# A two-layer encoder on one core: the casts, sums and embedding weights around the down projection, and when the first transposes follow

## The chip, the cores and the metric

The kernel runs on one core of a Trainium2 chip. Its time is device microseconds of one execution of the whole program; a version's time is the median of several runs. The engines are TensorE (PE in the profile, its weight loads PEld), VectorE (DVE), ScalarE (ACT), GpSimd (POOL) and SyncE (SP), which issues the transfers. Each engine takes its own instructions in the order of the program and waits on semaphores for what other engines make.

## What is computed

Two layers of an encoder on 1024 tokens of width 1024 in float32. The first layer's mixer is a pair of attentions, the second's a differential attention. The parts that the change touches come behind the mixer:

```python
def conv_ffn(x, w_gate, w_up, conv_w, conv_b, w_down):
    a = x @ w_gate
    u = x @ w_up
    ...
    return (jax.nn.gelu(c) * u) @ w_down      # c: a convolved over 3 tokens

x = layer_norm(ALPHA * x + mixer(x))
x = layer_norm(ALPHA * x + conv_ffn(x))
x = x + sigmoid(x @ W_g) * (p[i] @ W_p)       # the embedding step
```

The inner width of the feed-forward part is 2816, so w_down is 2816x1024: 22 blocks of 128 rows.

## The kernel before

Float32 products are made of rounded halves. A value is split into a hi part, which is a cast to a shorter format, and a lo part, the value less its hi part; `mm3` (lines 159 to 161) issues three matmuls, hi by hi, hi by lo and lo by hi. So each operand needs one cast (on ACT or POOL) and one subtraction (line 142, DVE, `lo_part`; line 149 in `split`).

**The down projection** (class `Down`) uses seven half-sized products instead of eight: `DOWN` lists them, a00, s4, a01, s2, s3, s1, a11. The left operand gr (combined gated activations, prepared before and kept in DRAM) and the right one wd (a block of w_down or a sum of two) are multiplied over nh = 11 blocks for each of the seven, so 77 products n per layer. A product is four blocks t of 128 tokens by 512 columns, three matmuls 128x512 each, so 12 matmuls. `run` goes through n in order; at n it issues the product's matmuls, then sums of weights for n + 5 (`draw`), then at most two steps that read a finished group's banks into xn (`read`, lines 1180 to 1201), then the operands of n + 3 (`prep`, AHEAD = 3): the cast of gr to gd (line 1149, ACT), the cast of wd (line 1150, through `pool_copy` at line 139, POOL), and two lo parts (line 142, DVE). `add` (line 319, DVE) makes the sums of weights in place, for s4 and a01 inside `prep`, for s2 and s3 in `draw`. gr comes by DMA on SP, two products in one transfer, into two buffers (`load_g`, line 1126). The operands gd and wd live in buffers for three products.

The last three products (74 to 76) are issued together for each token block: at n = 74 the loop goes over t, and for each t over the three products, so that the banks of a token block are done early.

**The embedding step** (class `Embedding`) is prepared beside the last group of products: `beside(f)` is called at the end of step f of group 6. It fetches the eight blocks of its weights (wgr), splits them into wgh and wgl (line 146 cast on ACT, line 149 lo part on DVE for even blocks and on POOL for odd ones), takes the statistics and the norm of the first token blocks (lines 892 to 897 statistics, 902 to 904 the norm's three steps), and at f = 7 puts the first transposes (`turn(0)`: eight matmuls by the identity at line 164, a cast at line 289 on ACT and lo parts on DVE). The products with W_g (pg) come behind the projection.

The order on each engine is set when the program is built: a scheduler takes the work that is ready by its costs and priorities, and an instruction named in `keep_in_program_order` stays where the program text has it. Step 74's loop is written before its `beside`, and f = 7 belongs to step 73, so the transposes stand ahead of product 74.

Of the kernel before, what the change touches and what calls it, by code (L numbers as in the profile page):

```python
# [12 lines left out]
ALU = mybir.AluOpType  # L13
# [4 lines left out]
NK = 8  # L18
NF = 22
# [13 lines left out]
def tile_hybrid_encoder(  # L33
# [32 lines left out]
    nc = tc.nc  # L66
# [61 lines left out]
    def f32(ap):  # L128
        return ap.bitcast(F32)
# [8 lines left out]
    def pool_copy(o, i):  # L138
        nc.gpsimd.tensor_scalar(o, i, 1.0, 1.0, op0=ALU.mult, op1=ALU.mult)  # L139
# [176 lines left out]
            return self.h[t][:, k, :], self.l[t][:, k, :]  # L316

    def add(o, a, b, op=ALU.add, eng=None):
        (eng or nc.vector).tensor_tensor(f32(o), f32(a), f32(b), op=op)

    def split_value(v, h, l, hi=None):
        if hi is nc.gpsimd:
# [776 lines left out]
    class Down:  # L1099
# [29 lines left out]
        def draw(self, n):  # L1129

            if n >= self.n:
                return
            q, f = DOWN[n // self.nh], n % self.nh
            b00, b01, b10, b11 = (self.b(f, kc) if f + self.nh * kc[0] in self.w else None
                                  for kc in ((0, 0), (0, 1), (1, 0), (1, 1)))
            if q == "s2":
                add(b00, b11, b00)
            if q == "s3":
                add(b10, b10, b00, ALU.subtract)

        def prep(self, n):

            if n >= self.n:
                return
            q, f = DOWN[n // self.nh], n % self.nh
            make = runit if q == "a11" else rtile
            g, w = make("gd", [P, 2, 512]), make("wd", [P, 2, 512])
            rg, rw = self.raw[n // 2][:, n % 2, :], self.b(f, self.B[q])
            nc.scalar.copy(g[:, 0], rg)  # L1149
            pool_copy(w[:, 0], rw)  # L1150
            lo_part(g[:, 1], rg, g[:, 0])
            lo_part(w[:, 1], rw, w[:, 0])
            if q == "s4":
                add(rw, rw, self.b(f, (0, 1)), ALU.subtract)
            if q == "a01":
                add(self.b(f, (0, 1)), self.b(f, (0, 1)), self.b(f, (0, 0)), ALU.subtract)
            self.op[n] = g, w
            if n % 2 == 1:
                self.load_g((n + 3) // 2)
# [60 lines left out]
        def run(self, beside):  # L1220
            nh, n_all = self.nh, self.n
            end = n_all - AHEAD
            for n in range(n_all):
                q, f = n // nh, n % nh
                if f == 0:
                    self.banks(q)
                if n < nh:
                    self.load_w(nh + n)
                if nh < n <= nh + 4:
                    residual(self.i, self.xns, n - nh - 1)  # L1230
                if 3 * nh < n <= 3 * nh + 4:
                    residual(self.i, self.xns, n - 3 * nh + 3)
                if n < end:
                    for t in range(4):
                        self.product(n, t)
                elif n == end:
                    for t in range(4):
                        for m in range(end, n_all):
                            self.product(m, t)
                        if t == 1:  # L1240
                            for step in self.read(q)[0:2]:
                                step()
                if n < end:
                    self.op.pop(n)
                self.draw(n + AHEAD + 2)
                for _ in range(2):
                    if self.todo:
                        self.todo.pop(0)()
                self.prep(n + AHEAD)
                if f == nh - 1 and q < 6:  # L1250
                    self.todo += self.read(q)
                if q == 6 and n < end:
                    beside(f)
            for step in self.read(6)[2:]:
                step()

# [262 lines left out]
    class Embedding:  # L1519
        def __init__(self, i, xns, sink):  # L1520
            self.i, self.xns, self.sink = i, xns, sink
            self.w, self.st, self.rows = [], {}, {}

        def load(self):

# [4 lines left out]
                    raw[k] = unit("wgr", [P, 1024])  # L1530
                    nc.sync.dma_start(out=raw[k], in_=w_ple[self.i, k])

            def weight(k):
                make = rtile if k < 3 else runit
                h, l = make("wgh", [P, 1024]), make("wgl", [P, 1024])
                split(raw.pop(k), h, l, nc.scalar, nc.gpsimd if k % 2 else nc.vector)
                self.w.append((h, l))

            def beside(n):
                if n == 0:  # L1540
                    self.ln = LN(ln_fg[self.i], ln_fb[self.i])
                    fetch(0)
                    fetch(1)
                if n > 0:
                    for k in ((0,), (1,), (2,), (3, 4), (5,), (6,), (7,))[n - 1] if n <= 7 else ():
                        fetch(k + 2)
                        weight(k)
                if n == 3:
                    self.stats(0, False)
                if n == 5:  # L1550
                    self.apply(0)
                if n == 6:
                    self.stats(1, False)
                if n == 7:
                    self.turn(0)
            return beside

# [162 lines left out]
```

## Time and profile before

| | |
|---|---|
| median of 3 runs | 3075.62 us (3073.82 to 3077.36) |
| the profiled execution | 3070.2 us, its span 3068.4 us |
| PE busy | 2956.1 us, 96% |
| DVE, ACT, POOL busy | 2339.5, 1239.0, 1110.6 us |
| one projection in the profile | about 1250 to 1472 us in layer 0, the like in layer 1 |

The profile is of one execution. Busy time counts instructions of an engine; where one waits, the timeline shows the idle before it in brackets with the instruction that released it. Matmuls overlap: in a full stream one starts each 0.227 us, though its row is 0.39 us long, so what a wait costs is read from start to start.

### The profile page before, as it was taken

To read this page: it belongs to the slowest core of one execution; us is meant where nothing else is said; L and a number is where in the kernel's file an instruction comes from. 1 tells how busy PE (TensorE), PEld (TensorE's weight loads), DVE (VectorE), ACT (ScalarE), POOL (GpSimd) and SP (SyncE) were. 2 spreads that over 40 slices of the span, in tenths; PEclk is the share of its full clock that TensorE was granted. 3 is DMA by queue.
4 is the path that set the end of the run, shared out by engine and by line. 5 is a ranking of instruction groups with operands and counts; after the bars stand their busy time and mean duration, and the time that the engine had idled before them with its cause. 6 is when DMAs were issued, how large, how long until landed. Compare 5 with 4: busy or idle time off the path is not lost.

```text
span 3068.4 us, 43192 instructions
## 1 busy us (share of the span) xinstructions
PE 2956.1 (96%) x15456; PEld 2535.4 (83%) x15456; DVE 2339.5 (76%) x4014; ACT 1239.0 (40%) x2652; POOL 1110.6 (36%) x1646
## 2 busy tenths in 40 slices
PE   8999999999889999999999999999998999999989
PEld 8888989887778888877788999998776888887877
DVE  6676477876898888788638777777779988879674
ACT  5555477761232222223226555555413322222221
POOL 4444544333232222234225555554333222213232
PEclk9999999999999999999999999999998999999999
DMA  3000100033223232734111100001532232255331
GB/s 122 29 28 19 38 29 8 22 118 130 96 103 103 99 106 106 283 112 168 56 59 36 35 28 29 28 18 62 174 108 86 103 103 103 103 201 198 97 137 65
DMA packets 119718, 272.14 MB, mean 89 GB/s; under 512 B 11344, under 2 KB 35024, under 8 KB 119504
## 3 DMA queue, kind: packets, MB, share of 16 engines
q1 hardware_dynamic: 119504, 269.37, 25.6%
q8 instruction: 123, 2.02, 0.3%
q14 instruction: 91, 0.75, 0.1%
HBM read 196.46 MB, written 72.88 MB: 88 GB/s over the span
## 4 chain that ended last, share of the span: by engine, by line
PE 70%; DVE 16%; issue 6%; POOL 3%; ACT 3%; DMA 2%; SPq 0%; POOLq 0%; DVEq 0%; ACTq 0%
PE xt L164 5%; PE pb L159 5%; PE pb L160 5%; PE pb L161 5%; PE pp L159 4%; PE s L588 4%; PE pp L161 4%; PE pp L160 4%; PE pd L160 2%; PE pd L161 2%; PE pd L159 2%; PE pa L159 2%; PE pg L159 2%; PE pa L161 2%; PE pa L160 2%
## 5 line engine op out<-in xcount | busy, mean ns | idle before, releaser
L142 DVE TENSOR_TENSOR ptl<-xt,pth 128x512 fp32r<-128x512 f32 (+2 forms) x384 | 239.7, 652 | 59.2 <-ACT pth L399 42.6
L159 PE MATMUL pp<-wh,xth 128*128 128x384 f32 x768 | 266.3, 347 | 7.9 <-ACT wh L146 7.4
L160 PE MATMUL pp<-wl,xth 128*128 128x384 f32 x768 | 258.8, 337 | 1.9 <-DVE wl L149 1.9
L161 PE MATMUL pp<-wh,xtl 128*128 128x384 f32 x768 | 257.9, 336 | 0.0
L440 ACT ACTIVATE e<-s,nmx 128x1024 f32<-128x1024 f32 x192 | 214.7, 1120 | 81.4 <-DVE nmx L838 58.7
L160 PE MATMUL pd<-wd,gd 128*128 128x512 f32 x616 | 242.4, 393 | 4.2 <-DVE wd L142 4.2
L159 PE MATMUL pd<-wd,gd 128*128 128x512 f32 x616 | 241.0, 391 | 0.0
L161 PE MATMUL pd<-wd,gd 128*128 128x512 f32 x616 | 240.5, 390 | 0.0
L139 POOL TENSOR_SCALAR wd<-wd 128x512 fp32r<-128x512 f32 x154 | 129.9, 848 | 290.8 <-PE pd L161 215.6
L1149 ACT CAST gd<-gr 128x512 fp32r<-128x512 f32 x154 | 94.8, 622 | 312.2 <-PE pd L161 222.0
L325 ACT CAST w<-ws 128x512 fp32r<-128x512 f32 x132 | 81.2, 621 | 336.8 <-PE pb L161 281.2
L164 PE MATMUL xt<-ident,e 128*128 128x128 f32 x1440 | 198.0, 274 | 10.0 <-POOL e L740 3.0
L159 PE MATMUL pb<-xt,w 128*128 128x512 f32 x528 | 207.0, 392 | 0.0
L160 PE MATMUL pb<-xt,w 128*128 128x512 f32 x528 | 206.5, 391 | 0.0
L161 PE MATMUL pb<-xt,w 128*128 128x512 f32 x528 | 206.3, 391 | 0.0
L139 POOL TENSOR_SCALAR w<-ws 128x512 fp32r<-128x512 f32 x44 | 33.4, 761 | 467.1 <-PE pa L161 416.9
L164 PEld LDWEIGHTS xt<-ident,e 128*128 128x128 f32 x1440 | 163.4, 141 | 30.7 <-ACT sq L870 5.9
L142 DVE TENSOR_TENSOR wd<-wd,wd 128x512 fp32r<-128x512 f32 x154 | 112.3, 731 | 68.8 <-POOL wd L139 68.8
L142 DVE TENSOR_TENSOR w<-ws,w 128x512 fp32r<-128x512 f32 x176 | 152.4, 869 | 5.2 <-ACT w L325 3.2
L159 PEld LDWEIGHTS pp<-wh,xth 128*128 128x128 f32 x768 | 144.6, 188 | 13.4 <-ACT wh L146 8.0
L838 DVE TENSOR_REDUCE nmx<-s 128x1 f32<-128x1024 f32 x128 | 150.4, 1213 | 1.7 <-PE s L588 1.6
L159 PE MATMUL pb<-xb,w 128*128 128x512 f32 x352 | 140.2, 398 | 9.8 <-DVE u L1330 5.7
(293 smaller groups left out, 8864.5 us busy)
## 6 DMA issues: line engine op xcount, KB each, us to landing
gr<-gated SPq DMA_DIRECT2D x76, 512.0 KB, 3.7
gated<-c SPq DMA_DIRECT2D x90, 256.0 KB, 3.7
wf<-in_w_gate_dram SPq DMA_DIRECT2D x44, 512.0 KB, 4.0
wf<-in_w_up_dram SPq DMA_DIRECT2D x44, 512.0 KB, 4.1
wd<-in_w_down_dram SPq DMA_DIRECT2D x44, 512.0 KB, 6.0
wr<-in_w_c_dram SPq DMA_DIRECT2D x32, 384.0 KB, 3.2
gated<-u SPq DMA_DIRECT2D x44, 256.0 KB, 2.2
pes<-peo SPq DMA_DIRECT2D x64, 128.0 KB, 1.9
```

The lines of the kernel that those rows point to most:

```text
L139: nc.gpsimd.tensor_scalar(o, i, 1.0, 1.0, op0=ALU.mult, op1=ALU.mult)
L142: nc.vector.tensor_tensor(lo, src, f32(hi), op=ALU.subtract)
L159: nc.tensor.matmul(o, lhsT=lh, rhs=rh, start=start, stop=False)
L160: nc.tensor.matmul(o, lhsT=lh, rhs=rl, start=False, stop=False)
L161: nc.tensor.matmul(o, lhsT=ll, rhs=rh, start=False, stop=stop)
L164: nc.tensor.transpose(o, in_=i, identity=ident)
L325: nc.scalar.copy(h, v)
L440: nc.scalar.activation(dst, s, AF.Exp, bias=negmax, scale=1.0, accum_out=l)
L588: nc.tensor.matmul(s[:, kh * 512:kh * 512 + 512], lhsT=qt[:, hl, i, :], rhs=self.ks[kh][:, j, :], start=hl == 0, stop=hl == 1)
L838: nc.vector.tensor_reduce(out=nmx, in_=s, axis=AX.X, op=ALU.max, negate=True)
L1149: nc.scalar.copy(g[:, 0], rg)
```

## The change

Five edits, in both layers alike. The cast of wd goes from POOL to ACT. The sums of weights are pinned to their place in the program. Weights 3 to 7 of the embedding are fetched beside group 5, and 3 to 6 split there, the rest beside group 6 at f = 0 and 2 to 4; every lo part of them is on DVE. The weights are held in a dict by their number. The transposes of the first token block are put in the last step's loop, ahead of its fourth token block.

```diff
--- before.py
+++ after.py
@@ -316,7 +316,7 @@
             return self.h[t][:, k, :], self.l[t][:, k, :]
 
     def add(o, a, b, op=ALU.add, eng=None):
-        (eng or nc.vector).tensor_tensor(f32(o), f32(a), f32(b), op=op)
+        return (eng or nc.vector).tensor_tensor(f32(o), f32(a), f32(b), op=op)
 
     def split_value(v, h, l, hi=None):
         if hi is nc.gpsimd:
@@ -1134,9 +1134,9 @@
             b00, b01, b10, b11 = (self.b(f, kc) if f + self.nh * kc[0] in self.w else None
                                   for kc in ((0, 0), (0, 1), (1, 0), (1, 1)))
             if q == "s2":
-                add(b00, b11, b00)
+                tc.keep_in_program_order(add(b00, b11, b00))
             if q == "s3":
-                add(b10, b10, b00, ALU.subtract)
+                tc.keep_in_program_order(add(b10, b10, b00, ALU.subtract))
 
         def prep(self, n):
 
@@ -1147,13 +1147,13 @@
             g, w = make("gd", [P, 2, 512]), make("wd", [P, 2, 512])
             rg, rw = self.raw[n // 2][:, n % 2, :], self.b(f, self.B[q])
             nc.scalar.copy(g[:, 0], rg)
-            pool_copy(w[:, 0], rw)
+            nc.scalar.copy(w[:, 0], rw)
             lo_part(g[:, 1], rg, g[:, 0])
             lo_part(w[:, 1], rw, w[:, 0])
             if q == "s4":
-                add(rw, rw, self.b(f, (0, 1)), ALU.subtract)
+                tc.keep_in_program_order(add(rw, rw, self.b(f, (0, 1)), ALU.subtract))
             if q == "a01":
-                add(self.b(f, (0, 1)), self.b(f, (0, 1)), self.b(f, (0, 0)), ALU.subtract)
+                tc.keep_in_program_order(add(self.b(f, (0, 1)), self.b(f, (0, 1)), self.b(f, (0, 0)), ALU.subtract))
             self.op[n] = g, w
             if n % 2 == 1:
                 self.load_g((n + 3) // 2)
@@ -1235,6 +1235,8 @@
                         self.product(n, t)
                 elif n == end:
                     for t in range(4):
+                        if t == 3:
+                            beside(nh)
                         for m in range(end, n_all):
                             self.product(m, t)
                         if t == 1:
@@ -1249,8 +1251,8 @@
                 self.prep(n + AHEAD)
                 if f == nh - 1 and q < 6:
                     self.todo += self.read(q)
-                if q == 6 and n < end:
-                    beside(f)
+                if q >= 5 and n < end:
+                    beside(f if q == 6 else f - nh)
             for step in self.read(6)[2:]:
                 step()
 
@@ -1519,7 +1521,7 @@
     class Embedding:
         def __init__(self, i, xns, sink):
             self.i, self.xns, self.sink = i, xns, sink
-            self.w, self.st, self.rows = [], {}, {}
+            self.w, self.st, self.rows = {}, {}, {}
 
         def load(self):
 
@@ -1530,28 +1532,32 @@
                     raw[k] = unit("wgr", [P, 1024])
                     nc.sync.dma_start(out=raw[k], in_=w_ple[self.i, k])
 
-            def weight(k):
-                make = rtile if k < 3 else runit
+            def weight(k, make=runit):
                 h, l = make("wgh", [P, 1024]), make("wgl", [P, 1024])
-                split(raw.pop(k), h, l, nc.scalar, nc.gpsimd if k % 2 else nc.vector)
-                self.w.append((h, l))
+                split(raw.pop(k), h, l, nc.scalar)
+                self.w[k] = h, l
 
             def beside(n):
+
+                if -11 < n < 0 and n % 2 == 0:
+                    fetch(NK + n // 2)
+                if -10 < n < -2 and n % 2 == 1:
+                    weight(NK + (n - 1) // 2)
                 if n == 0:
+                    weight(7)
                     self.ln = LN(ln_fg[self.i], ln_fb[self.i])
                     fetch(0)
-                    fetch(1)
-                if n > 0:
-                    for k in ((0,), (1,), (2,), (3, 4), (5,), (6,), (7,))[n - 1] if n <= 7 else ():
-                        fetch(k + 2)
-                        weight(k)
+                if n in (1, 2):
+                    fetch(n)
+                if n in (2, 3, 4):
+                    weight(n - 2, rtile)
                 if n == 3:
                     self.stats(0, False)
                 if n == 5:
                     self.apply(0)
                 if n == 6:
                     self.stats(1, False)
-                if n == 7:
+                if n == NF // 2:
                     self.turn(0)
             return beside
 
```

What this does to the order of each engine's instructions is seen at three places of layer 0. The first is PE at the last products: pd are the banks of token blocks, wd and gd the operands, xt the transposes' banks. Before:

```order
L159 MATMUL pd_15070<-wd_15203,gd_15202 128x512
L160 MATMUL pd_15070<-wd_15203,gd_15202 128x512
L161 MATMUL pd_15070<-wd_15203,gd_15202 128x512
L164 MATMUL xt_15305<-ident,xn_13945 128x128 x4
L164 MATMUL xt_15312<-ident,xn_13945 128x128 x4
L159 MATMUL pd_15069<-wd_15235,gd_15234 128x512
L160 MATMUL pd_15069<-wd_15235,gd_15234 128x512
```

After:

```order
L159 MATMUL pd_15096<-wd_15298,gd_15297 128x512
L160 MATMUL pd_15096<-wd_15298,gd_15297 128x512
L161 MATMUL pd_15096<-wd_15298,gd_15297 128x512
L164 MATMUL xt_15334<-ident,xn_13945 128x128 x4
L164 MATMUL xt_15341<-ident,xn_13945 128x128 x4
L159 MATMUL pd_15096<-wd_15249,gd_15248 128x512
L160 MATMUL pd_15096<-wd_15249,gd_15248 128x512
```

The eight transposes (two rows of four) stood ahead of product 74's first matmul and stand now behind three of its four token blocks, 27 matmuls later.

The second is DVE while the first sums of weights are made: line 142 are the lo parts, line 319 the sums. Before:

```order
L319 TENSOR_TENSOR wd_13683<-wd_13683,wd_13536 128x512
L319 TENSOR_TENSOR wd_13536<-wd_13536 128x512
L319 TENSOR_TENSOR wd_13536<-wd_13683,wd_13536 128x512
L142 TENSOR_TENSOR gd_13888<-gr_13829,gd_13888 128x512
L142 TENSOR_TENSOR wd_13889<-wd_13705,wd_13889 128x512
L319 TENSOR_TENSOR wd_13705<-wd_13705,wd_13538 128x512
L319 TENSOR_TENSOR wd_13538<-wd_13538 128x512
L142 TENSOR_TENSOR gd_13909<-gr_13829,gd_13909 128x512
L142 TENSOR_TENSOR wd_13910<-wd_13725,wd_13910 128x512
L319 TENSOR_TENSOR wd_13538<-wd_13705,wd_13538 128x512
L319 TENSOR_TENSOR wd_13725<-wd_13725,wd_13554 128x512
L319 TENSOR_TENSOR wd_13554<-wd_13554 128x512
```

After, once each sum is pinned:

```order
L142 TENSOR_TENSOR gd_14003<-gr_13916,gd_14003 128x512
L142 TENSOR_TENSOR wd_14004<-wd_13809,wd_14004 128x512
L319 TENSOR_TENSOR wd_13809<-wd_13809,wd_13597 128x512
L142 TENSOR_TENSOR gd_14026<-gr_13966,gd_14026 128x512
L142 TENSOR_TENSOR wd_14027<-wd_13831,wd_14027 128x512
L319 TENSOR_TENSOR wd_13831<-wd_13831,wd_13599 128x512
L142 TENSOR_TENSOR gd_14045<-gr_13966,gd_14045 128x512
L142 TENSOR_TENSOR wd_14046<-wd_13851,wd_14046 128x512
L319 TENSOR_TENSOR wd_13851<-wd_13851,wd_13617 128x512
```

Two or three sums stood together between pairs of lo parts; one stands behind each pair now.

The third is DVE at the end of the projection: wgl are the lo parts of embedding weights, st and mv the statistics, xn with lngb the norm. Before, up to the lo part of the last but one weight:

```order
L142 TENSOR_TENSOR gd_15202<-gr_15091,gd_15202 128x512
L895 BN_AGGR mv_15183<-st_15182 128x2
L142 TENSOR_TENSOR wd_15203<-wd_13831,wd_15203 128x512
L902 TENSOR_SCALAR xn_13945<-xn_13945,mv_15183,rs_15184 128x1024
L149 TENSOR_TENSOR wgl_15219<-wgr_15174,wgh_15218 128x1024
L142 TENSOR_TENSOR gd_15234<-gr_15146,gd_15234 128x512
L142 TENSOR_TENSOR wd_15235<-wd_13851,wd_15235 128x512
L903 TENSOR_TENSOR xn_13945<-xn_13945,lngb_15093 128x1024
L142 TENSOR_TENSOR gd_15261<-gr_15146,gd_15261 128x512
L904 TENSOR_TENSOR xn_13945<-xn_13945,lngb_15093 128x1024
L142 TENSOR_TENSOR wd_15262<-wd_13874,wd_15262 128x512
L149 TENSOR_TENSOR wgl_15268<-wgr_15216,wgh_15267 128x1024
```

After, the rows that hold the same lo parts:

```order
L149 TENSOR_TENSOR wgl_15233<-wgr_15172,wgh_15232 128x1024
L142 TENSOR_TENSOR gd_15248<-gr_15170,gd_15248 128x512
L142 TENSOR_TENSOR wd_15249<-wd_13851,wd_15249 128x512
L902 TENSOR_SCALAR xn_13945<-xn_13945,mv_15205,rs_15206 128x1024
L142 TENSOR_TENSOR gd_15269<-gr_15170,gd_15269 128x512
L903 TENSOR_TENSOR xn_13945<-xn_13945,lngb_15123 128x1024
L142 TENSOR_TENSOR wd_15270<-wd_13874,wd_15270 128x512
L904 TENSOR_TENSOR xn_13945<-xn_13945,lngb_15123 128x1024
L892 BN_STATS st_15277<-xn_13968 128x6
L142 TENSOR_TENSOR gd_15297<-gr_15230,gd_15297 128x512
L895 BN_AGGR mv_15278<-st_15277 128x2
L142 TENSOR_TENSOR wd_15298<-wd_13895,wd_15298 128x512
```

The norm's last step (line 904) had two of the lo parts of wd and one of an embedding weight behind it; now the embedding's are all ahead of it, and the last pair of gd and wd alone is behind it with the second block's statistics.

On ACT 77 casts at line 1150 per layer are added, each behind the cast of its gd, and on POOL the 77 at line 139 and four of line 149 are gone.

## Rows read from the trace of the kernel before

**Rows 1.** of the page: busy time by engine, then two groups of instructions.

```profile
PE 2956.1 (96%) x15456; PEld 2535.4 (83%) x15456; DVE 2339.5 (76%) x4014; ACT 1239.0 (40%) x2652; POOL 1110.6 (36%) x1646
...
L139 POOL TENSOR_SCALAR wd<-wd 128x512 fp32r<-128x512 f32 x154 | 129.9, 848 | 290.8 <-PE pd L161 215.6
L1149 ACT CAST gd<-gr 128x512 fp32r<-128x512 f32 x154 | 94.8, 622 | 312.2 <-PE pd L161 222.0
```

**Rows 2.** PE's waits, 1230 to 1520 us, layer 0 (us in total, times, longest).

```profile
PE xt L164 <- DVE xn L904: 7.0, 1, 7.0
PE pd L160 <- DVE wd L142: 2.1, 5, 0.5
```

**Rows 3.** PE's waits, 2720 us to the end, layer 1.

```profile
PE xt L164 <- DVE xn L904: 8.6, 1, 8.6
```

**Rows 4.** PE's timeline at weight stalls: start, length, instruction [idle before, releaser].

```profile
1299.81 0.39 PE L159 MATMUL pd<-wd,gd 128*128 128x512 f32 x1
1300.70 0.50 PE L160 MATMUL pd<-wd,gd 128*128 128x512 f32 x1 [0.51 <-DVE wd L142]
1301.04 0.39 PE L161 MATMUL pd<-wd,gd 128*128 128x512 f32 x1
...
1328.45 0.50 PE L160 MATMUL pd<-wd,gd 128*128 128x512 f32 x1 [0.40 <-DVE wd L142]
```

**Rows 5.** PE's timeline at the first transposes, layer 0.

```profile
1453.24 0.39 PE L161 MATMUL pd<-wd,gd 128*128 128x512 f32 x1
1460.65 1.97 PE L164 MATMUL xt<-ident,xn 128*128 128x128 f32 x8 [7.02 <-DVE xn L904]
1462.28 0.78 PE L159 MATMUL pd<-wd,gd 128*128 128x512 f32 x1
...
1464.87 0.39 PE L159 MATMUL pd<-wd,gd 128*128 128x512 f32 x1
```

**Rows 6.** PE's timeline, the same place in layer 1.

```profile
2955.66 1.97 PE L164 MATMUL xt<-ident,xn 128*128 128x128 f32 x8 [8.55 <-DVE xn L904]
```

**Rows 7.** DVE's timeline at the end of the projection, layer 0.

```profile
1431.53 1.28 DVE L1180 TENSOR_TENSOR xn<-xn,pd 128x512 f32<-128x512 f32 x2
...
1436.33 1.21 DVE L149 TENSOR_TENSOR wgl<-wgr,wgh 128x1024 fp32r<-128x1024 f32 x1
...
1438.66 1.71 DVE L142 TENSOR_TENSOR gd<-gr,gd 128x512 fp32r<-128x512 f32 x1
...
1449.12 1.11 DVE L902 TENSOR_SCALAR xn<-xn,mv,rs 128x1024 f32<-128x1024 f32 x1 [0.72 <-POOL rs L897]
1450.15 3.41 DVE L149 TENSOR_TENSOR wgl<-wgr,wgh 128x1024 fp32r<-128x1024 f32 x1
...
1455.51 3.35 DVE L903 TENSOR_TENSOR xn<-xn,lngb 128x1024 f32<-128x1024 f32 x1
...
1460.52 0.68 DVE L142 TENSOR_TENSOR wd<-wd,wd 128x512 fp32r<-128x512 f32 x1
...
1463.58 0.63 DVE L142 TENSOR_TENSOR wd<-wd,wd 128x512 fp32r<-128x512 f32 x1
```

**Rows 8.** POOL's timeline in the same stretch.

```profile
1437.00 2.82 POOL L149 TENSOR_TENSOR wgl<-wgr,wgh 128x1024 fp32r<-128x1024 f32 x1 [7.84 <-ACT wgh L146]
...
1449.64 2.83 POOL L149 TENSOR_TENSOR wgl<-wgr,wgh 128x1024 fp32r<-128x1024 f32 x1
```

**Rows 9.** ACT's timeline at the start of that stretch.

```profile
1430.27 1.14 ACT L1149 CAST gd<-gr 128x512 fp32r<-128x512 f32 x2 [4.65 <-DMA gr<-gated]
```

**Rows 10.** by windows: us, each engine's busy time, PE clock, DMA share, GB/s.

```profile
1440.00:1460.00 20.00, 13.63 (x61) 10.95 (x59) 19.28 (x18) 6.93 (x8) 14.01 (x10) 0.95 0.62 230
```

**Rows 11.** of the page: fetches of gr (KB each, median us to landing).

```profile
gr<-gated SPq DMA_DIRECT2D x76, 512.0 KB, 3.7
```

**Rows 12.** groups of instructions on DVE, 1310 to 1430 us: line 1201.

```profile
L1201 DVE SCALAR_TENSOR_TENSOR xn<-xn,V 128x1024 f32<-128x1024 f32 x4 | 5.6, 1422 | 0.0
```

## Prediction

> **What bounds the kernel now.** I began with the page: PE is busy 2956.1 of 3068.4 us, DVE 2339.5, ACT 1239.0, POOL 1110.6 [rows 1]. The kernel is bound by the matrix engine, so a change to the casts, the sums and the order can gain only what PE loses while it waits. Next I asked PE for its waits in the stretch that holds a down projection, once per layer. Layer 0 shows two kinds: one wait of 7.0 us of the first transposes for the last step of the layer norm (line 904), and five waits of a product for the lo part of its weight (line 142), 2.1 us together [rows 2]. Layer 1 has 8.6 us of the first kind [rows 3], and of the second a row that reads the same. So the places are known; the next view, PE's timeline, gives their size.
>
> Matmuls of a product start every 0.227 us, though a row lasts 0.39, so the idle that a row shows is less than what is lost. From start to start, the first weight stall takes 0.89 us before the matmul that waited and 0.34 before the next, in place of 0.227 each [rows 4]. There are six such places in layer 0, the last at 1328.45; all twelve gaps less 0.227 each make 3.70 us, and the same sum in layer 1 makes 3.48. The transposes start at 1460.65, 7.41 us after the matmul ahead of them, a loss of 7.18; then six matmuls take from 1462.28 to 1464.87, 2.59 us where full speed takes 1.36, a loss of 1.23 [rows 5]. The row of 0.78 behind the idle against 0.39 ahead of it says which level that is: after the seven idle microseconds the clock stood at 1.2 GHz, and it came back to 2.4. Layer 1 has the same with 8.55 us of idle [rows 6]; from start to start that is 8.71, and again 1.23. Layer 0 loses 3.70 + 7.18 + 1.23 = 12.1 us, layer 1 loses 3.48 + 8.71 + 1.23 = 13.4. **The ceiling of the gain is 25.5 us.**
>
> Why DVE is late at the end I read from its timeline. From the first read of the product before (1431.53) to the end of the lo part of the last product's weight (1463.58 + 0.63) DVE runs 32.7 us nearly without idle [rows 7]. Many rows there are longer than others of the same form: a weight's lo part of 128x1024 takes 1.21 at 1436.33 and 3.41 at 1450.15, line 903 of the same size takes 3.35 at 1455.51, a lo part of 128x512 1.71 at 1438.66; two reads of that size take 1.28 at 1431.53. Each long row lies beside a POOL instruction [rows 8]; over the eight long rows, from 1438.66 to 1455.51, the excess sums to 8.5 us. Besides, 0.72 us passes in a wait for POOL's line 897, ahead of 1449.12.
>
> **The change part by part.**
>
> Hi casts of the weights from POOL to ACT. 154 casts of 848 ns leave POOL [rows 1]; nothing of that is on PE's path by itself. ACT gets 154, and a second cast behind a first costs 1.14 - 0.62 = 0.52 us: two in a row take 1.14 [rows 9], one alone 622 ns [rows 1]. Per product ACT then works 1.14 of 2.72 us (12 matmuls of 0.227). ACT is 40% busy over the span and 6.93 of 20 us in this stretch [rows 10], so 154 x 0.52 = 80 us lies beside PE's work. What could bring it onto the path is order, not load: ACT takes its queue in turn, so a cast of a weight that is ready now stands behind a cast of gr whose transfer has not landed (ACT waited 4.65 us for one [rows 9]). Behind that cast wait DVE's two lo parts, and behind these the fetch of the next gr. Two buffers of gr hold two products each, so a loop of four products, 10.9 us, has to hold one landing, 3.7 us in the median [rows 11], two pairs of casts (2.28) and the lo parts (1.3): 7.3. There is 3.6 us of room; cost nothing on average, and if one landing takes over 7.3 us, the excess.
>
> Weight sums held in program order. As many sums remain; before they stood in bunches of two and three between lo parts, and the stalls of [rows 4] lie in just that place. After, lo, lo, sum repeats: three times 0.60, and where two reads of a product join, 3.0 us of DVE against 2.72 of a product. An operand is made three products ahead, so a lag of a few tenths for some products is absorbed. I take the weight stalls as gone: -3.70 and -3.48. Bounds: 0, and -7.2 together.
>
> The embedding's weights. Four lo parts per layer leave POOL for DVE: they cost POOL 2.8 us each [rows 8], DVE 1.14 to the next start each (1.21 long [rows 7]). Four of the eight are now made beside the last product group but one, where DVE then has eleven pairs of lo parts (13.2), eight reads (4.8), four of line 1201 (5.6 [rows 12]) and these four (4.56): 28.2 us in 29.9 of PE. That fits if the fetches, five of which now queue on SP between those of gr, don't hold it. Bounds: 0, and one late landing per layer at 4.65 us, ACT's wait of [rows 9].
>
> The end. Counted from the first read, DVE's list up to the last weight's lo part has now eight reads (8 x 0.60 = 4.8), sixteen lo parts (9.6), four lo parts of embedding weights (4.56), two halves of statistics and two aggregates (1.44), and of the norm of the first block 0.73 + 1.20 + 1.13 = 3.06. Sum 23.5 us at the rows' undisturbed lengths, where the old list took 32.7. Started at 1431.53 it ends at 1455.0. PE reached product 74's place at 1453.47 (1453.24 + 0.23 [rows 5]); there come six matmuls (1.36) and one more (0.23): it wants the last lo part at 1455.1. So it fits, with nothing to spare. The transposes come 27 matmuls (6.1 us) later than before and then wait for nothing, since line 904 now stands ahead of the last lo parts. Note what moving them alone would do: the lo parts of the last two weights ended at 1461.2 and 1464.2 in the old order [rows 7], so PE would have stopped for these instead. It is the shorter DVE list that makes the move worth something. With no idle, the slow clock after it goes as well. Taken: -7.18 - 1.23 and -8.71 - 1.23, +0.3 for the tight fit in each layer, and for layer 1 +1.4 more, because DVE runs later against PE there: its stall is longer by 1.5 us, 8.55 against 7.02 [rows 5, 6], and of this I let most stay. For late landings in either layer I add 0.5 each.
>
> SBUF is where a rule is to be weighed against these rows. The DMA share in 1440 to 1460, where the long rows are, is 0.62 [rows 10], so traffic could be the cause of long DVE rows as well as POOL. The Trainium skill ("SBUF — State Buffer", Who interferes with whom) says that transfers don't contend with a compute engine, and that a VectorE instruction with two inputs in SBUF contends with a GpSimd one that reads SBUF, one of them blocking for as long as the other holds the ports. By it all 8.5 us of excess goes with POOL's work; if traffic were the cause it would stay, which is the first rival. By that rule the trace agrees: the long rows lie beside POOL's [rows 7, 8].
>
> **Sum.** -25.5 + 0.6 + 1.4 + 1.0 = -22.5 us: 3070.2 of the profiled execution becomes 3047.7. The runs' median, 3075.62, is 5.4 above that execution; I carry this over: **3053 us**.
>
> **Rivals.**
> (a) DVE's end stays late, because its long rows come from traffic or because the weights' fetches arrive late: the 8.5 us of excess remains in each layer as a stall on the last weights' lo parts. Gain 25.5 - 17 = 8.5: 3067. For: DMA share 0.62. Against: the pairing with POOL, row by row.
> (b) The weight stalls stay or only move: beside the last group but one ACT's casts wait for fetches, and three DVE steps with two reads exceed 2.72 for longer than three products' lead covers. For: 28.2 of 29.9 us. Against: only the four of line 1201 are longer than the rest. Gain 25.5 - 7.2 - 3 = 15.3: 3060.
> (c) Slower: the loop of gr decides. Both casts now stand in one queue, so each pair of products lengthens the loop by 1.04 us. If landings reach 7.3 us as a rule, PE follows the loop, and 154 x 0.52 = 80 us comes on the path: 3075.6 + 80 - 25.5 = 3130. It decides from 7.3 us of landing; the median is half of that, and only where other transfers share the queues can it be near.
> (d) The change doesn't do what it says: the stall of 7 to 9 us simply moves to the transposes' new place or to the first product of the embedding, and waits for gr eat the rest: within 6 us of before, some 3072. For: DVE ends at 1455.0 where PE wants it at 1455.1. Against: the stall has two causes, and both are touched.
>
> **How the numbers follow.** Forecast 0.66 (3049 to 3058 on its own), (b) 0.13, (a) 0.10, (d) 0.06, (c) 0.05. Below the ceiling's 3050 only the spread of the runs (3.5 us) remains, so the range begins at 3047; upward it takes in (b) and (a), to 3069. A measurement of this kernel can tell about 0.2%, 6 us, from no change: faster is the forecast, (b) and (a) less 0.03 for the worst of (a), 0.86; no change is (d) and 0.02 of that, 0.08; slower is (c) and 0.01, 0.06.
>
> **What would show it.** PE's waits in the two stretches have neither line 904 nor a weight's lo part above 0.5 us; the transposes' row starts with PE at full clock, no row of 0.78 behind it. DVE's rows of lines 142, 149 and 903 keep 0.68 and 1.21 in the last 25 us of each projection. ACT has about 154 casts more and stays under half busy. POOL loses some 150 us. Wrong would be: a wait of PE for a lo part in the end stretch (a), waits of line 1149 or 1150 for gr that return to PE all through the projection (c), stalls where the sums are (b).

## The result, and the profile after

The changed kernel takes 3049.41 us in the median of four runs (3047.42 to 3053.64), the kernel before 3076.02 in its four: a ratio of 0.9916 (95% interval 0.9899 to 0.9933), 26.6 us less. The forecast was 3053 us, and 3047 to 3069 as the range. The profiled execution of the changed kernel has a span of 3045.1 us, 23.3 less than the one before.

The page's first line beside that of [rows 1]: PE is busy 6.9 us less, in a span that is 23.3 us shorter: most of what went is idle time.

```profile
PE 2949.2 (97%) x15456; PEld 2533.8 (83%) x15456; DVE 2308.2 (76%) x4022; ACT 1318.1 (43%) x2806; POOL 963.6 (32%) x1484
```

In groups of lines on ACT, the casts of wd (line 1150) stand beside those of gr: 154 of each, 0.62 us each, and only 11.9 us of idle ahead of the second of all pairs.

```profile
L1149 ACT CAST gd<-gr 128x512 fp32r<-128x512 f32 x154 | 96.0, 623 | 214.9 <-PE pd L161 176.1 <-DMA gr<-gated 20.7 <-PE pb L161 11.5
L1150 ACT CAST wd<-wd 128x512 fp32r<-128x512 f32 x154 | 94.8, 615 | 11.9 <-PE pb L161 8.4 <-DVE wd L142 2.5 <-DVE wgl L149 1.0
```

PE's waits in layer 0's stretch, the view of [rows 2] (us in total, times, longest):

```profile
PE pg L161 <- DVE xtl L142: 0.8, 1, 0.8
PE pd L160 <- DVE wd L142: 0.2, 1, 0.2
```

Neither line 904 nor the weight stalls of the early groups are there; layer 1 shows the same wait for xtl and for its weights none. PE's timeline at the end of the projection (start, length, instruction, in brackets the idle and its releaser), the place of [rows 5]:

```profile
1450.07 0.39 PE L159 MATMUL pd<-wd,gd 128*128 128x512 f32 x1
1450.68 0.50 PE L160 MATMUL pd<-wd,gd 128*128 128x512 f32 x1 [0.22 <-DVE wd L142]
...
1455.39 1.03 PE L164 MATMUL xt<-ident,xn 128*128 128x128 f32 x8
1456.18 0.48 PE L159 MATMUL pd<-wd,gd 128*128 128x512 f32 x1
...
1458.55 0.39 PE L160 MATMUL pg<-wgl,xth 128*128 128x512 f32 x1
1459.73 0.50 PE L161 MATMUL pg<-wgh,xtl 128*128 128x512 f32 x1 [0.79 <-DVE xtl L142]
```

The transposes start without idle, 1.03 us for eight as against 1.97, and no slow matmul follows. Two small losses are left: the last weight's lo part comes 0.5 us late (0.61 and 0.34 between starts in place of 0.227 each), and the first W_g product waits for xtl (1459.73 - 1458.55 = 1.18, 0.95 too much). DVE's timeline of the stretch of [rows 7]:

```profile
1427.26 1.28 DVE L1180 TENSOR_TENSOR xn<-xn,pd 128x512 f32<-128x512 f32 x2
...
1429.66 1.22 DVE L149 TENSOR_TENSOR wgl<-wgr,wgh 128x1024 fp32r<-128x1024 f32 x1
...
1445.80 1.22 DVE L903 TENSOR_TENSOR xn<-xn,lngb 128x1024 f32<-128x1024 f32 x1
...
1447.54 1.22 DVE L904 TENSOR_TENSOR xn<-xn,lngb 128x1024 f32<-128x1024 f32 x1
...
1449.99 0.64 DVE L142 TENSOR_TENSOR wd<-wd,wd 128x512 fp32r<-128x512 f32 x1
```

The list from the first read to the last lo part takes 1449.99 + 0.64 - 1427.26 = 23.4 us, where it took 32.7. All rows have their short length: 1.22 for a weight's lo part and for line 903, not 3.41 and 3.35. And traffic is there all the same (windows: DMA share is the last but one):

```profile
1430.00:1450.00 20.00, 20.00 (x90) 16.57 (x89) 20.00 (x31) 10.53 (x17) 1.93 (x2) 1.00 0.68 245
```

Since the profiled executions differ by up to 5.6 us outside the projections (from the first W_g product of layer 0 to the next projection, 1269.9 to 1275.5 us), the experiments are read by one more number: the time from the start of the first matmul of the projection (pd) to the start of the first W_g product (pg), read from PE's timeline of each profiled execution. It repeats within 0.2 us (the changed kernel profiled again: 210.7 and 210.5).

| kernel | layer 0 | layer 1 | median of runs, us | ratio to before, 95% |
|---|---|---|---|---|
| before | 223.6 | 225.2 | 3076.0 to 3076.9 | 1 |
| changed | 210.9 | 210.5 | 3049.4 | 0.9916 (0.9899 to 0.9933) |
| transposes moved, alone | 225.7 | 227.8 | 3081.5 | 1.0014 (1.0005 to 1.0023) |
| casts on ACT, alone | 219.6 | 218.3 | 3062.2 | 0.9949 (0.9937 to 0.9962) |
| lo parts on DVE, alone | 217.2 | 218.8 | 3062.1 | 0.9954 (0.9941 to 0.9966) |
| these two | 211.6 | 211.6 | 3048.9 | 0.9910 (0.9897 to 0.9924) |
| changed, casts back on POOL | 215.4 | 216.8 | 3059.0 | 0.9940 (0.9928 to 0.9953) |
| changed, odd lo parts back on POOL | 215.7 | 215.5 | 3061.5 | 0.9949 (0.9935 to 0.9962) |
| changed, sums not pinned | 210.8 | 210.4 | 3049.3 | 0.9911 (0.9897 to 0.9924) |
| changed, weights split late | 211.6 | 212.0 | 3049.2 | 0.9906 (0.9892 to 0.9920) |
| changed, transposes back | 210.4 | 210.4 | 3047.4 | 0.9904 (0.9890 to 0.9917) |
| changed, sums not pinned and transposes back | 210.5 | 210.4 | 3044.2 | 0.9895 (0.9880 to 0.9910) |
| transposes back, POOL additions added | 219.9 | 220.4 | 3067.5 | 0.9966 (0.9952 to 0.9979) |

### The profile page after: what moved, and what is told of

It is laid out like the page before. It is cut to its first block, busy times and chain, and to the rows that moved or that the text cites. A ratio compares the mean times of both kernels' runs of the same rounds, so it can differ in the third digit from the quotient of the medians.

```text
span 3045.1 us, 42940 instructions
## 1 busy us (share of the span) xinstructions
PE 2949.2 (97%) x15456; PEld 2533.8 (83%) x15456; DVE 2308.2 (76%) x4022; ACT 1318.1 (43%) x2806; POOL 963.6 (32%) x1484
## 4 chain that ended last, share of the span: by engine, by line
PE 74%; DVE 15%; ACT 3%; issue 3%; POOL 3%; DMA 2%; SPq 0%; DVEq 0%; ACTq 0%; POOLq 0%
PE pb L159 5%; PE pb L161 5%; PE pb L160 5%; PE xt L164 5%; PE pp L159 4%; PE s L588 4%; PE pp L161 4%; PE pp L160 4%; PE pd L159 4%; PE pd L161 4%; PE pd L160 4%; PE pa L159 2%; PE pg L159 2%; PE pg L161 2%; PE pg L160 2%
## 5 line engine op out<-in xcount | busy, mean ns | idle before, releaser
L896 POOL TENSOR_SCALAR rs<-mv 128x1 f32<-128x1 f32 x32 | 9.3, 291 | 547.7 <-DVE mv L895 547.1
L142 DVE TENSOR_TENSOR gd<-gr,gd 128x512 fp32r<-128x512 f32 x154 | 106.1, 689 | 77.1 <-ACT gd L1149 77.1
```

What stands on the lines that cost most here:

```text
L142: nc.vector.tensor_tensor(lo, src, f32(hi), op=ALU.subtract)
L896: nc.gpsimd.tensor_scalar(rs, mv[:, 1:2], 1.0, LN_EPS, op0=ALU.mult, op1=ALU.add)
```

## The experiments

**Does the transposes' place matter?** First their move alone, on the kernel before:

```diff
                     for t in range(4):
+                        if t == 3:
+                            beside(nh)
                         for m in range(end, n_all):
...
-                if n == 7:
+                if n == NF // 2:
                     self.turn(0)
```

> The kernel before with one edit alone: the first transposes moved 27 matmuls later. My theory: DVE's list at the end is too long, and the transposes' wait only hid that the lo parts of the last two weights are late too. DVE's order up to them is the same, so they end at 1461.2 and 1464.2 in layer 0 as before; PE wants them at about 1454.4 and, after the first stall, 1461.9. Stalls of about 6.8 and 2.3 us take the place of the 7.2, the clock still falls, layer 1 likewise 1.5 us later: 3074 to 3079 us, no gain (0 plus or minus 3). Rival: the transposes' place was the cause; the stall goes and with it the slow clock, 16 to 18 us, about 3058.

3081.5 us: not a gain but 4 to 5 us more (1.0014 of the kernel before; 4.7 us in the two projections). PE's timeline in layer 0:

```profile
1456.88 0.50 PE L160 MATMUL pd<-wd,gd 128*128 128x512 f32 x1 [2.27 <-DVE wd L142]
...
1462.51 0.79 PE L160 MATMUL pd<-wd,gd 128*128 128x512 f32 x1 [4.67 <-DVE wd L142]
...
1465.52 0.80 PE L160 MATMUL pd<-wd,gd 128*128 128x512 f32 x1 [1.36 <-DVE wd L142]
```

The wait has changed its name. In the place of one stall for line 904 stand three for lo parts of the last three weights, 2.27 + 4.67 + 1.36 = 8.3 us, with the slow clock behind the second (a row of 0.79, then rows of 0.63). The theory had two stalls, of 6.8 and 2.3; I had overlooked that the weight of product 74 was late too: its lo part ended at 1455.6 in the kernel before. So a wait of PE names who is last there, not who is late.

Then the other way, the changed kernel without the move:

```diff
-                        if t == 3:
-                            beside(nh)
...
-                if n == NF // 2:
+                if n == 7:
                     self.turn(0)
```

> The changed kernel with the transposes put back ahead of product 74; nothing else differs on any engine but where their own eight matmuls, casts and lo parts stand. My theory: with DVE's short list line 904 ends at about 1448.8 and PE comes to that place at 1448.7, so the transposes wait 0.2 to 0.5 us per layer, the clock does not fall, and the xtl wait of 0.8 us goes as well: 3047 to 3052, the same as the changed kernel. The move is then worth nothing beside the rest. Rival: the move is needed; a wait of 5 to 9 us for line 904 comes back in each layer, 3060 to 3068.

3047.4 us, and PE has no wait at all in layer 0's stretch: neither for line 904 nor for xtl, since the lo parts of xt now have 36 matmuls of cover. The move does not help with the rest in place, and costs 0.5 us at layer 0's last lo part and 1.1 in each layer at the first W_g product.

**Do the pinned sums matter?** In the changed kernel the four sums lose their pin:

```diff
-                tc.keep_in_program_order(add(b00, b11, b00))
+                add(b00, b11, b00)
...
```

> The changed kernel with the four sums of weights no longer held in program order. Theory as in the prediction: the bunches of two and three sums between lo parts make the weight stalls, so they return, 3.5 us per layer: 3055 to 3058. Rival: with the casts off POOL the DVE rows there are 0.60 and the cast is ready earlier, so a bunch is absorbed by the lead of three products: 3048 to 3051, PE's row for line 142 under 0.5 us in each layer.

3049.3 us and projections of 210.8 and 210.4: no weight stall came back, so the rival holds and my step falls. DVE's groups in 1290 to 1330, where the stalls of [rows 4] were, in the kernel before (count, busy, mean ns):

```profile
L319 DVE TENSOR_TENSOR wd<-wd,wd 128x512 f32<-128x512 f32 x21 | 15.5, 771 | 0.0
...
L319 DVE TENSOR_TENSOR wd<-wd 128x512 f32<-128x512 f32 x7 | 6.3, 917 | 0.0
```

and in this run:

```profile
L319 DVE TENSOR_TENSOR wd<-wd,wd 128x512 f32<-128x512 f32 x23 | 15.0, 686 | 0.1
...
L319 DVE TENSOR_TENSOR wd<-wd 128x512 f32<-128x512 f32 x7 | 4.8, 684 | 0.0
```

The sums are bunched in both (in this run three stand together from 1295.93 to 1297.82). Before, with POOL's casts beside them, they took 771 and 917 ns in the mean; without a POOL instruction beside them they take 0.68 us. In the run with the casts back on POOL but with the pins (below) the weight stalls are absent as well, and in the run with the casts alone on ACT and no pins too. Either edit removes them; both were made, and each alone would have done.

**POOL's casts.** All of the change but this:

```diff
-            nc.scalar.copy(w[:, 0], rw)
+            pool_copy(w[:, 0], rw)
```

> The changed kernel with the hi casts of wd back on POOL, all else as changed. My theory (DVE is slowed by POOL's instructions that read SBUF): with POOL's casts of 0.85 us beside them, one DVE row per product is 0.4 us longer; over the last nine products that is 3 to 4 us more DVE work in a list that just fits, so a stall of 2 to 4 us per layer on the last lo parts, and 0 to 2 us of weight stalls: 3053 to 3060. Rival: only POOL's long lo parts of 2.8 us mattered; then 3048 to 3051, and no row of wd's lo parts decides.

3059.0 us, in the theory's range, with PE's wait where it was put:

```profile
PE pd L160 <- DVE wd L142: 2.9, 2, 2.0
```

The way there was only partly the one expected. In the last stretch two of DVE's rows are longer by 0.4 us each, 0.8 in all. The rest had begun earlier: DVE reached its first read 2.4 us after PE had begun the group, as against 0.3 in the changed kernel, and ACT shows what for, two casts of gr that waited for late fetches:

```profile
1424.13 1.15 ACT L1149 CAST gd<-gr 128x512 fp32r<-128x512 f32 x2 [5.22 <-DMA gr<-gated]
...
1430.09 1.14 ACT L1149 CAST gd<-gr 128x512 fp32r<-128x512 f32 x2 [3.35 <-DMA gr<-gated]
```

0.8 + 2.1 = 2.9 us, the wait above. That DVE's longer rows held those fetches back (SP issues one behind a lo part of gd) fits the order, and was not tried by itself.

And the casts alone on the kernel before, the same line the other way round:

> The kernel before with one edit alone: the hi casts of wd on ACT. Theory: the weight stalls go (7.2 us in both layers), since a late cast and slow DVE rows made them; in the last stretch POOL's four lo parts of 2.8 us per layer remain, each still holding a DVE row for about 2 us, so line 904 is late by 3 to 5 us less than before and the transposes still wait 3 to 6 us per layer: 3060 to 3066. Rival: the casts are the whole matter, 3050 to 3054; or they are nothing by themselves, 3072 to 3076.

3062.2 us, as the theory had it. In layer 0 PE still stops three times:

```profile
1454.77 1.10 PE L164 MATMUL xt<-ident,xn 128*128 128x128 f32 x8 [2.82 <-DVE xn L904]
...
1458.17 0.50 PE L160 MATMUL pd<-wd,gd 128*128 128x512 f32 x1 [1.37 <-DVE wd L142]
...
1460.51 0.79 PE L160 MATMUL pd<-wd,gd 128*128 128x512 f32 x1 [1.36 <-DVE wd L142]
```

POOL's lo parts of 2.4 to 3.0 us are still there, and DVE's row beside one (POOL's ran from 1450.59 to 1453.03) is four times its length:

```profile
1450.72 2.86 DVE L142 TENSOR_TENSOR wd<-wd,wd 128x512 fp32r<-128x512 f32 x1
```

**POOL's lo parts.** In the changed kernel the odd ones go back:

```diff
-                split(raw.pop(k), h, l, nc.scalar)
+                split(raw.pop(k), h, l, nc.scalar, nc.gpsimd if k % 2 else nc.vector)
```

> The changed kernel with the lo parts of the odd embedding weights back on POOL (two of them beside the last group of products, two beside the one before). Theory: a POOL lo part of 2.8 us holds one DVE row for about 2.2 us, more than the 1.14 us that DVE saves, so giving work to POOL makes DVE later by about 1 us for each; two in the last stretch, 2 us per layer on the last lo part or line 904: 3051 to 3055. Rival: DVE is relieved, its list is 2.3 us shorter, the small waits of the changed kernel go: 3045 to 3048.

3061.5 us: the direction was the theory's, the size was not: 12 us where it put 2 to 6. POOL's row and DVE's beside it:

```profile
1433.04 2.79 POOL L149 TENSOR_TENSOR wgl<-wgr,wgh 128x1024 fp32r<-128x1024 f32 x1 [14.64 <-DVE xn L1180]
```

```profile
1433.49 2.88 DVE L142 TENSOR_TENSOR wd<-wd,wd 128x512 fp32r<-128x512 f32 x1
```

POOL's ends at 1435.83 and DVE's 0.54 us later, as if it had begun its own work then: 2.88 - 0.68 = 2.2 us lost for 1.14 saved, as expected per piece (the other piece of the last group lost 1.7: 2.40 in place of 0.68). The price was set too low, since I had put nothing for the slow clock behind the stall, for xtl, which is then late by 1.8 us, and for a late start: DVE's first read came 1.9 us after PE had begun the last group, as against 0.3 in the changed kernel, with two long rows (1.88 and 2.89) in the group before.

POOL can be the one that is held, too. In the group before the last one of its lo parts took 10.69 us:

```profile
1404.89 10.69 POOL L149 TENSOR_TENSOR wgl<-wgr,wgh 128x1024 fp32r<-128x1024 f32 x1 [178.71 <-ACT wgh L146]
```

DVE's rows beside it kept 0.69 and 1.22 and followed each other without a gap until 1413.30; POOL's ended 2.3 us after that. Layer 1 has a row of 10.69 us at the same place. Why POOL's got in at once at 1433 and had to stand back here isn't shown.

The lo parts alone on the kernel before (the diff above with its sign turned):

> The kernel before with one edit alone: all lo parts of embedding weights on DVE; the casts of wd stay on POOL. Theory: the weight stalls stay, 7.2 us in both layers; at the end POOL's casts still hold one DVE row of a product by 0.4 us, and the list has four lo parts more but none of POOL's of 2.8 us: 30 us in place of 32.7, so the end still costs 3 to 6 us per layer: 3062 to 3070. Rival: only POOL's lo parts mattered at the end, and 3055 to 3060 comes out.

3062.1 us, the lower edge of the theory's range. PE's waits in layer 0:

```profile
PE pd L160 <- DVE wd L142: 2.5, 6, 0.5
PE xt L164 <- DVE xn L904: 1.7, 1, 1.7
```

The weight stalls stay (five of the six waits for line 142; the sixth, 0.4 us, is at the end). They cost 3.7 us from start to start, as before, so the end of layer 0 costs 217.2 - 210.4 - 3.7 = 3.1 us where it cost 9.5. It costs DVE four more instructions per layer and is a gain of 14 us.

**These two together and nothing else**, on the kernel before:

> The kernel before with two edits alone: the casts of wd on ACT and all lo parts of embedding weights on DVE. Sums not pinned, weights fetched and split where they were, transposes as written before. Theory: freeing DVE of POOL's reads is the whole of the gain; the longer DVE list (four lo parts more, 4.6 us) costs a stall of about 1 to 2 us per layer at the end, since the scheduler now puts matmuls of the next token block ahead of the late lo parts: 3049 to 3054. Rival: the move of four weights to the group before is needed as well, 5 us per layer: 3057 to 3062.

3048.9 us, the changed kernel's time within what can be told, and 423.2 us of both projections against 421.4. The two waits that are left:

```profile
1452.62 1.09 PE L164 MATMUL xt<-ident,xn 128*128 128x128 f32 x8 [0.50 <-DVE xn L904]
...
1456.22 0.50 PE L160 MATMUL pd<-wd,gd 128*128 128x512 f32 x1 [0.22 <-DVE wd L142]
```

So the other edits are not needed for the gain. One caution: here, as in the run with lo parts alone, the scheduler wrote PE's last products in another order (the next token block's matmuls ahead of those that want a late lo part), so some of DVE's four extra lo parts is hidden by that.

**The weights split beside the group before.** The changed kernel with all eight weights back in the last group:

```diff
-                if q >= 5 and n < end:
-                    beside(f if q == 6 else f - nh)
+                if q == 6 and n < end:
+                    beside(f)
```

> The changed kernel with the fetch and split of all eight embedding weights back beside the last group of products, as before the change, but every lo part on DVE. Theory: DVE's list up to the last weight's lo part grows by four lo parts of 1.14 us, 4.6 us, from a list that just fits; the last lo parts are 4.5 to 5 us late in each layer and the clock falls after it (1 us): 3058 to 3062. Rival: the move of the four weights was not needed, since the leads of three products take it up: 3048 to 3052.

3049.2 us: my expectation missed. The wait that was to be 4.5 to 5 us is 0.6:

```profile
1452.64 0.50 PE L160 MATMUL pd<-wd,gd 128*128 128x512 f32 x1 [0.61 <-DVE wd L142]
```

DVE's list did grow, to 27.3 us; but the scheduler moved PE's order as in the run before this. This does not measure the edit alone, since two things changed, and says only that with the scheduler free the move is worth 0.7 and 1.5 us of projection time.

**POOL's reads by themselves.** To the version with the transposes back one POOL instruction per product of the last group is added:

```diff
+            if q == "a11":
+                nc.gpsimd.tensor_tensor(f32(self.b(f, (1, 1))), f32(g[:, 0]), f32(w[:, 0]), op=ALU.add)
             self.op[n] = g, w
```

> The changed kernel with the transposes at their old place (the run that showed no wait in the projection), and one added POOL addition of 128x512 per product of the last group, which reads the hi parts of the two operands from SBUF and writes a half of a weight that is no longer used; its result goes nowhere. DVE's order is the same, and no transfer is added. Theory (DVE's rows with two SBUF inputs are held by POOL's reads): rows of 0.68 beside it become 1.1 to 1.9, rows of 1.22 become 1.6 to 2.5; with eleven of them DVE is 4 to 9 us later at line 904, PE waits for it in each layer: 3056 to 3068. Rival (traffic made the long rows of before): DVE's rows keep 0.68 and 1.22, 3045 to 3050.

3067.5 us, 20 us for 22 additions whose result nobody reads (19.5 in the two projections). DVE's groups in 1428 to 1460, first of this run:

```profile
L142 DVE TENSOR_TENSOR wd<-wd,wd 128x512 fp32r<-128x512 f32 x9 | 9.4, 1042 | 0.0
L142 DVE TENSOR_TENSOR gd<-gr,gd 128x512 fp32r<-128x512 f32 x9 | 9.3, 1037 | 0.8 <-ACT gd L1149 0.8
L1182 DVE TENSOR_TENSOR xn<-xn,pd 128x512 f32<-128x512 f32 x8 | 5.1, 676 | 0.0
...
L902 DVE TENSOR_SCALAR xn<-xn,mv,rs 128x1024 f32<-128x1024 f32 x1 | 1.8, 1758 | 0.0
```

then of the changed kernel:

```profile
L1180 DVE TENSOR_TENSOR xn<-xn,pd 128x512 f32<-128x512 f32 x9 | 5.8, 679 | 0.0
L142 DVE TENSOR_TENSOR gd<-gr,gd 128x512 fp32r<-128x512 f32 x8 | 5.4, 680 | 0.0
L142 DVE TENSOR_TENSOR wd<-wd,wd 128x512 fp32r<-128x512 f32 x8 | 5.4, 670 | 0.0
...
L902 DVE TENSOR_SCALAR xn<-xn,mv,rs 128x1024 f32<-128x1024 f32 x3 | 2.4, 810 | 1.7 <-POOL rs L897 1.7
```

Lo parts rise from 0.68 to 1.04 in the mean, line 902 from 0.81 to 1.76, while the reads of banks (line 1182 here, 1180 there) keep theirs. The addition also writes SBUF, so its reads and its writes aren't told apart here. PE then waits as it did before, with the slow clock behind it:

```profile
1459.74 1.97 PE L164 MATMUL xt<-ident,xn 128*128 128x128 f32 x8 [5.76 <-DVE xn L904]
1461.36 0.78 PE L159 MATMUL pd<-wd,gd 128*128 128x512 f32 x1
```

**Both idle edits undone**, the pins and the transposes' move (their diffs are above):

> The changed kernel with both edits undone that were worth nothing one by one: sums not pinned, transposes ahead of product 74. Theory: they don't cover for each other, no wait of PE in the projection: 3045 to 3050, the least of all versions with the run that only put the transposes back. Rival: one stood in for the other, and weight stalls or a wait for line 904 come back: 3053 to 3060.

3044.2 us (3043.42 to 3045.17), the least of all, with no wait of PE in layer 0's projection. On the same chip the changed kernel once more:

> The changed kernel once more, to stand beside the run without pins and with the transposes put back on the same chip: 3048 to 3051. Waits of 0.2 and 0.8 us per layer at the end, about 3 us in both layers from start to start with what follows them, make it 1 to 3 us slower than that run, if the difference can be told at all.

3049.0 us (3047.49 to 3050.41). The four runs of each do not overlap; the difference is 4.8 us, more than the 1 to 3 expected. The waits removed come to 2.5 us from start to start in the two profiles (0.2 in layer 0, 0.1 in layer 1, 1.1 in each at the W_g product). Of the 5.5 us between the two profiled spans 1.5 lie ahead of layer 0's projection, where no edit reaches; so what of the 4.8 us beyond 2.5 belongs to the edits isn't shown.

## Why the prediction was right

**The ceiling** was the step that was mis-sized. I found 25.5 us of loss; by the table the projections took 223.6 + 225.2 where 210.4 each is reached without a wait, so 28.0. Of the missing 2.5 us, 1.7 are the eight transposes themselves, which ran at the lower clock too: 1462.28 - 1460.65 = 1.63 us [rows 5] against 1456.18 - 1455.39 = 0.79 in the changed kernel, 0.84 more in each layer. I had counted the slow clock for the matmuls behind them alone. Another 0.2 is in layer 1's weight stalls: the twelve gaps make 3.70 there as in layer 0, not 3.48. The last 0.6 isn't traced to a place. The changed kernel gained 27.4 of the 28.0.

**The residue** was nearly right in sum, 3.0 forecast and 2.8 found, and wrong in its parts: I had let 1.4 us of layer 1's lateness stay, and none did: DVE's first read came 1.35 us after PE began the last group there in the kernel before, and 0.07 ahead of it in the changed one. The wait for xtl (1.1 us in each layer) was in no term.

**The end** held, term by term: a DVE list of 23.5 us was forecast and 23.4 found; the last lo part was to be just in time and was up to 0.5 us late. That the move of the transposes alone would only rename the stall held too. But I did not draw the conclusion from my own numbers: the list of 23.5 us less the four rows behind line 904 (1.9), begun at 1431.53, ends at 1453.1, ahead of PE at 1453.47. In the changed kernel line 904 was done at 1448.76 and PE at product 74 at 1448.71. So the move wasn't needed either, and the 18 us that I credited to the end, move and shorter list together, were paid by DVE's shorter list alone.

**The weight stalls** went as forecast, but for half of a reason. I put them to the bunches of sums alone; the run without pins keeps the bunches and has no stall, so it took the bunches and POOL's casts together. A sum of 1.09 us in their midst and POOL's cast of about 1 us beside it stood in the trace of the kernel before, and I had counted such excess only at the end:

```profile
1304.00 1.09 DVE L319 TENSOR_TENSOR wd<-wd 128x512 f32<-128x512 f32 x1
```

```profile
1303.58 0.97 POOL L139 TENSOR_SCALAR wd<-wd 128x512 fp32r<-128x512 f32 x1 [2.45 <-PE pd L161]
```

So the total is right partly by luck. The pins and the move, which the sum credits with 7.2 us and with their part in the 18, were worth nothing beside the rest; the casts' move, of which it said that nothing lies on PE's path by itself, and the move of the lo parts, which it booked as work for DVE, bring the gain alone, by way of the long DVE rows that it rightly put to POOL. All five edits came in one change, so the total could not tell them apart.

**ACT's queue** was taken at nothing, which held: ACT's waits for gr fell in the projection of layer 0 from 28.2 us to 11.4.

**Rivals.** (a), DVE late through traffic, is refuted: a DMA share of 0.68 with every DVE row short, and long rows again with POOL's additions and no added transfer. The rule of the Trainium skill ("SBUF — State Buffer", Who interferes with whom) that a VectorE instruction with two inputs in SBUF meets GpSimd's reads, and one with an input elsewhere doesn't, is borne out by the additions: 0.68 to 1.04 us in the mean for the lo parts of gd and wd, 0.68 kept by the reads of banks. The section's rule that a tensor_scalar can enter a two-port mode, and then contends as well, would cover line 902 (0.81 to 1.76); whether line 902 was in that mode no run here shows. (b) kept none of its 7.2 us, (c) and (d) did not come near.

## What to carry to other kernels

When one engine's rows of one form have two lengths, look first at what another engine was doing beside the long ones: here it was worth 27 us, in two moves of work off GpSimd, though VectorE was the busier engine and got some of that work. A wait of the bound engine names only who was last; before moving the waiting instruction, look up when the next things that it needs were ready. And measure a stage from its first to its last instruction, not as a sum of the waits that the profile lists, since a slow clock and short gaps are in no wait.

## What the runs showed of the hardware

A POOL addition of 128x512 (1.3 us) lengthened a DVE lo part of 0.68 us to as much as 1.8, and line 902, with one tensor input of 128x1024, from 0.81 to 1.76. A POOL lo part of 128x1024 took 2.4 to 3.0 us where it got in at once, and DVE's lo part beside it 1.7 to 2.9 where 0.68 is its own. DVE's row ended 0.54 to 0.56 us behind POOL's: at 1436.37 against 1435.83 with the odd lo parts back, at 1453.58 against 1453.03 with the casts alone. So a held DVE row lasts until POOL's instruction ends and its own work comes behind that. In one place of each layer, beside DVE rows that followed each other without a gap, POOL's lo part was held instead, 10.69 us; what decides which of the two is held isn't shown. I had not counted on line 902, which reads one tensor.

After stalls of 4.67 and 5.76 us PE's clock was at its lower level (1.2 GHz, rows of 0.79 and 0.78; granted clock 0.50 behind the second). After one of 2.82 us in the run with casts alone the transposes took 1.10 and the matmul behind them 0.48, and the granted clock was 1.00, so the clock had stayed up; it fell only behind the third stall there (0.79 at 1460.51, granted 0.50). With the casts back on POOL a stall of 2.04 us, behind one of 0.83, was followed by a row of 0.80 at 1455.63 and a granted clock of 0.51. So the length of one stall by itself did not tell whether the clock fell.
